# A fused decoder layer on one core: the second feed-forward block computed with seven products in all eight row-tile pairs

## The chip, the core and the metric

The kernel runs on one core of one Trainium2 chip. The metric is the time of one execution on the device, in microseconds (us), as the median of several runs. The core has five engines with an instruction queue each, worked through in order: PE (matrix products), DVE (vector), ACT (activation, copies), POOL (GpSimd, here mostly issuing transfers) and SP (issuing transfers). An instruction that has to wait for another engine or for a transfer holds up everything behind it in its own queue.

## The reference

One decoder layer on 256 tokens of width 2048, all in float32. The change touches only the last line, the feed-forward part (`D_FF` is 5632):

```python
n = rms_norm(x, attn_norm_g)
proj = n @ w_in
...
h = x + jnp.concatenate([gla_out, nsa_out], axis=-1) @ w_out
m = rms_norm(h, ffn_norm_g)
return h + (jax.nn.silu(m @ w_gate) * (m @ w_up)) @ w_down
```

## The kernel before

**Precision.** Each float32 operand is split into two parts that the matrix unit takes: `hi`, which ACT writes by a copy, and `lo`, which DVE writes as operand minus `hi` (`in_parts`, lines 661 and 662). A product of two operands takes three matmuls: hi by hi, hi by lo, lo by hi. So every weight tile costs ACT and DVE a pass each before PE can use it.

**Feed-forward part.** The columns of `w_gate` and `w_up` are cut in 11 blocks of 512 (`FB`). The main loop (line 1424) runs `gate_up(f)` for a block and then `down(f - 1)`, the product of the block before with `w_down`; block 0 has no `down` behind it, so block 1 follows block 0 directly. The 2048 rows of the weights are 16 tiles of 128, taken as 8 pairs. A pair holds two gate tiles and two up tiles of 128 by 512, and is multiplied with two row tiles of 128 tokens. There are two ways to do that:

- Plain: 2 by 2 by 2, that is 8 products, 24 matmuls. Four weight tiles are split (one copy and one subtraction of 128 by 2048 elements).
- Seven products (a fast 2-by-2 multiplication): 21 matmuls. It needs three raw tiles split (128 by 1536), and four sums of weight tiles split (two passes of 128 by 1024 each on ACT and DVE, `parts_of2`). The token side needs sums too, the "forms", made once for each pair and kept (`pair_forms`).

**Where the four sums of a pair come from.** There are three ways. DVE makes them in the block (lines 1229 to 1231: one pass of 128 by 1024, two of 128 by 512). Or they were made early, on DVE during the earlier stages, stored in DRAM ("sums", `SUMS`), and are fetched by two POOL transfers (line 1172). Or two of the four are made by a transfer that adds (`HALVES`, `fetch_half`): POOL fetches a gate tile and an up tile into one buffer (lines 1182 and 1183), waits until both have landed, and issues a third transfer that adds the other up tile to both (line 1184); DVE makes the other two sums from the result (lines 1230 and 1231).

**Block 1 before.** `FIRST7` gives five pairs the seven products (0, 2, 3, 4, 5) and leaves 1, 6 and 7 plain; the order of pairs is 0, 1, 2, 6, 3, 4, 5, 7 (`ORDER1`). The sums of 2, 3, 4 and 5 come from DRAM, those of 0 are made on DVE. Later blocks do all eight pairs with seven products in plain order, two pairs with sums from DRAM (4 and 7), two with halves (2 and 6). The seven products of all pairs are summed in seven of the eight PSUM banks; plain pairs also need bank 8. So `turn_act(0)`, which transposes block 0's result for `down(0)` into a bank, uses banks 1 and 5 once these are read, after block 1's last seven-product pair; in later blocks it uses bank 8 at the start of the block.

**Buffers.** Raw weights have 4 buffers (`fraw`), split weights 4 (`ftwo`, two for a seven-product pair), sums 3 (`fsum`). A pool of 24 buffers, `g4`, holds everything else: 4 for the residual `h`, 8 for the tokens in two parts, one for the forms of each pair (6 before block 1; pairs 6 and 7 follow during block 1, `late_forms`, with a scratch buffer each), 2 for the transposed result of a block, and what is left serves sums from DRAM, halves, and sums made on DVE in blocks 0 and 1. A scheduler places the instructions of the program on the five queues; it interleaves pairs where operands are late. Transfers of a half keep the written order.

Of the kernel before, what the change touches and what calls it, by code (L numbers as in the profile page):

```python
# [37 lines left out]
def kernel(  # L38
# [986 lines left out]

    PAIRS7, FIRST7 = tuple(range(8)), {0: (0, 2, 4), 1: (0, 2, 3, 4, 5)}

    EARLY7 = (0,1,2,3,4,5)  # L1030
# [157 lines left out]
    def gate_up(fb):  # L1188
# [9 lines left out]
            assert k in turned  # L1198
            return tuple(x[k // 4][:, k % 4, t * P:(t + 1) * P] for x in (hT_h, hT_l))

        order, sevens = (ORDER0, ORDER1, ORDER)[min(fb, 2)], FIRST7.get(fb, PAIRS7)
        last7 = max(sevens, key=order.index)
        todo = dict.fromkeys((1, 5, 6, 7), 3 * len(sevens))
        todo.update(dict.fromkeys((2, 3, 4), 3 * len(sevens) + 6 * (8 - len(sevens))))
        todo[8] = 6 * (8 - len(sevens))
        total = dict(todo)
        if fb > 1:
            urgent.append(turn_act(fb - 1, (8, 8)))
        for at, pair in enumerate(order):
# [44 lines left out]
            if pair == last7:  # L1254
                (q1, q7u), (u, q5u), (q57u, _) = ((t[:, 0], t[:, 1]) for t in (fw["sum"]([2, 512]) for _ in range(3)))
                act(q1, banks[1], AF.Copy)
                TT(u, banks[6], q1, ALU.add)  # L1257
                TT(q5u, banks[5], u, ALU.subtract)
                TT(q7u, banks[7], u, ALU.add)
                TT(q57u, banks[5], q7u, ALU.subtract)  # L1260
                if fb == 1:
                    urgent.append(turn_act(0, (1, 5)))
                if fb:
                    seed(0, DOWN[min(fb - 1, 1)])
        if fb == 0:
            drain(urgent)
            rms(rf, ssh)
# [35 lines left out]

    DOWN = ((6, 7), (2, 3), (6, 7), (4, 8)), ((1, 6), (7, 5), (2, 3), (4, 1))

    def seed(n, qs):
        for t in range(NT):
            last["seed", n] = nc.scalar.copy(banks[qs[n][t]], h_sb[n][:, t, :])  # L1310

    def down(f):
        ah, al = acts.pop(f)
        qs = DOWN[min(f, 1)]
        for n in range(4):
            bs = [banks[q] for q in qs[n]]
            ws = parts_of(load4([(w_down[0], 4 * f, 4, n * 512)]), last["seed", 0] if n == 2 and f else None)
            if n < 3 and (f or n != 1):
                seed(n + 1, qs)
# [145 lines left out]
```

## Time and profile before

| | |
|---|---|
| median of 3 runs | 1095.55 us (1095.54 to 1096.16) |
| profiled execution, its own time | 1095.91 us |
| its span, first to last instruction | 1094.2 us |
| PE busy | 1088.2 us, 99% |
| DVE busy | 988.4 us, 90% |
| ACT busy | 764.7 us, 70% |
| POOL busy | 129.2 us, 12% |
| granted TensorE clock | 1.000 |

The profile is of one execution. A group row names line, engine, operation, output and inputs, shape and count, then busy time, mean duration of one in ns, and the idle time before it with what ended it. A windows row gives each engine's busy time in a stretch of the span and the number of instructions in brackets, the clock, the busy share of the DMA engines and what they moved. A timeline row gives start, duration, engine and instruction; neighbours of a kind are merged.

### The profile page before, as it was taken

How to read it: one execution, taken by the hardware profiler on the slowest of the kernel's cores; microseconds unless marked ns; L12 is line 12 of the kernel's file. 1: busy time of each engine (PE TensorE's matmuls, PEld its weight loads, DVE VectorE, ACT ScalarE, POOL GpSimd, SP SyncE). 2: the span in 40 equal slices, each digit the busy share in tenths (PEclk: the TensorE clock that was granted, in tenths of full speed). 3: DMA queues.
4: the chain of work that ended last, by engine and by line, in shares of the span. 5: the costliest groups of instructions: out<-in, count | busy, mean ns of one | idle time of the engine just before them, and what ended most of it. 6: DMA issues, size and time to landing. Idle time of an engine off the chain costs nothing.

```text
span 1094.2 us, 14835 instructions
## 1 busy us (share of the span) xinstructions
PE 1088.2 (99%) x5256; PEld 895.3 (82%) x5256; DVE 988.4 (90%) x1316; ACT 764.7 (70%) x1060; POOL 129.2 (12%) x213
## 2 busy tenths in 40 slices
PE   9999999999999999999999999999999999999998
PEld 8888888987878877888888888888888887888877
DVE  6768879987799888997999999999999999999997
ACT  7745557555687586677686967777686877777695
POOL 4100001032110100010101011010101011110100
PEclk9999999999999999999999999999999999999999
DMA  7999978468876947696787969787797869788862
GB/s 278 357 356 350 398 251 295 166 232 287 308 274 252 342 153 287 216 336 208 250 278 221 299 200 302 246 266 236 261 288 236 280 207 288 227 279 255 247 231 78
DMA packets 135272, 287.76 MB, mean 263 GB/s; under 512 B 8135, under 2 KB 10219, under 8 KB 135197
## 3 DMA queue, kind: packets, MB, share of 16 engines
q1 hardware_dynamic: 112844, 218.17, 57.4%
q0 software_dynamic: 21744, 68.17, 20.4%
q8 instruction: 41, 0.67, 0.2%
q10 hardware_dynamic: 608, 0.47, 0.1%
q14 instruction: 35, 0.28, 0.1%
HBM read 263.71 MB, written 23.07 MB: 262 GB/s over the span
## 4 chain that ended last, share of the span: by engine, by line
PE 85%; DVE 6%; issue 3%; ACT 2%; DMA 2%; POOL 1%; SPq 0%; DVEq 0%; POOLq 0%; ACTq 0%
PE bank L297 41%; PE bank L1194 37%; PE bank L215 3%; PE bank L1339 2%; DVE lo L145 2%; PE bank L977 1%; DMA fraw<-in_w_up_dram 1%; DMA g<-in_w_up_dram 1%; POOL sm L218 1%; DMA sums<-g 1%; ACT g L912 1%; DVE ftwo L662 0%; DVE g L1115 0%; ACT hi L144 0%; PE bank L899 0%
## 5 line engine op out<-in xcount | busy, mean ns | idle before, releaser
L1194 PE MATMUL bank<-ftwo,g 128*128 128x512 f32 x1824 | 427.1, 393 | 0.5 <-ACT ftwo L661 0.2
L1194 PEld LDWEIGHTS bank<-ftwo,g 128*128 128x128 f32 x1824 | 337.2, 188 | 77.5 <-ACT ftwo L661 3.2
L297 PE MATMUL bank<-hi,g 128*128 128x512 f32 (+1 forms) x1088 | 320.9, 376 | 0.4 <-ACT g L912 0.4
L662 DVE TENSOR_TENSOR ftwo<-fraw,ftwo 128x1536 fp32r<-128x1536 f32 (+1 forms) x130 | 253.0, 1952 | 4.7 <-ACT ftwo L661 4.7
L661 ACT ACTIVATE ftwo<-fraw 128x1536 fp32r<-128x1536 f32 (+1 forms) x130 | 212.5, 1641 | 17.5 <-PE bank L1194 14.4
L297 PE MATMUL bank<-ftwo,g 128*128 128x512 f32 x960 | 221.6, 391 | 0.0
L297 PEld LDWEIGHTS bank<-hi,g 128*128 128x128 f32 x1088 | 191.5, 188 | 31.0 <-issue 1.0
L297 PEld LDWEIGHTS bank<-ftwo,g 128*128 128x128 f32 x960 | 179.3, 188 | 39.5 <-ACT bank L1310 1.2
L297 PE MATMUL bank<-lo,g 128*128 128x512 f32 (+3 forms) x544 | 193.0, 375 | 0.1
L144 ACT ACTIVATE hi<-raw 128x1024 fp32r<-128x1024 f32 (+3 forms) x124 | 130.5, 1059 | 82.8 <-PE bank L297 56.0
L145 DVE TENSOR_TENSOR lo<-raw,hi 128x1024 fp32r<-128x1024 f32 (+3 forms) x124 | 150.2, 1219 | 30.3 <-ACT hi L144 29.7
L661 ACT ACTIVATE ftwo<-fsum 128x1024 fp32r<-128x1024 f32 x118 | 121.9, 1054 | 70.6 <-DVE fsum L1229 53.6
L662 DVE TENSOR_TENSOR ftwo<-fsum,ftwo 128x1024 fp32r<-128x1024 f32 x118 | 142.0, 1221 | 13.7 <-ACT ftwo L661 13.7
L297 PEld LDWEIGHTS bank<-lo,g 128*128 128x128 f32 x544 | 98.2, 189 | 14.5 <-DVE lo L145 0.3
L661 ACT ACTIVATE ftwo<-g 128x1024 fp32r<-128x1024 f32 x46 | 48.7, 1059 | 35.8 <-PE bank L1194 23.3
L1322 ACT COPY g<-bank 128x512 f32<-128x512 f32 x80 | 45.6, 583 | 27.8 <-PE bank L297 26.4
L662 DVE TENSOR_TENSOR ftwo<-g,ftwo 128x1024 fp32r<-128x1024 f32 x46 | 56.2, 1221 | 2.2 <-ACT ftwo L661 2.2
L1119 POOL DMA_DIRECT2D sums<-g x40 | 21.8, 545 | 260.1 <-DVE g L1115 206.3
L1310 ACT COPY bank<-g 128x512 f32<-128x512 f32 x80 | 45.1, 589 | 7.6 <-DVE fsum L1257 6.2
L1229 DVE TENSOR_TENSOR fsum<-fraw 128x1024 f32<-128x1024 f32 x36 | 44.0, 1223 | 0.1
L215 PE MATMUL bank<-ident,g 128*128 128x128 f32 (+3 forms) x232 | 42.6, 277 | 0.6 <-ACT g L912 0.5
L1231 DVE TENSOR_TENSOR fsum<-fsum,fraw 128x512 f32<-128x512 f32 x60 | 41.4, 689 | 1.0
(251 smaller groups left out, 951.8 us busy)
## 6 DMA issues: line engine op xcount, KB each, us to landing
fraw<-in_w_gate_dram SPq DMA_DIRECT2D x86, 512.0 KB, 4.4
fraw<-in_w_down_dram SPq DMA_DIRECT2D x42, 1024.0 KB, 6.8
raw<-in_w_in_dram SPq DMA_DIRECT2D x36, 1024.0 KB, 6.1
fraw<-in_w_up_dram SPq DMA_DIRECT2D x45, 512.0 KB, 5.4
sums<-g POOLq DMA_DIRECT2D x40, 512.0 KB, 6.6
raw<-in_w_out_dram SPq DMA_DIRECT2D x16, 1024.0 KB, 8.5
g<-in_w_up_dram POOLq DMA_DIRECT2D x21, 512.0 KB, 7.6
fraw<-in_w_up_dram SPq DMA_DIRECT2D x41, 256.0 KB, 4.3
```

Of the source, the lines that this page charges most:

```text
L144: act(h[:, i:i + n], r[:, k + i:k + i + n], AF.Copy)
L145: last["d"] = TT(o[:, i:i + n], r[:, k + i:k + i + n], f32(h[:, i:i + n]), ALU.subtract)
L215: return nc.tensor.transpose(o, i, ident[:n, :n])
L297: last["mm"] = mm(bk[t], a[:, k, t * P:(t + 1) * P], ws[k][m][:, off:off + w], start=(first_ and k == 0 and i == 0), stop=(end and k == 3 ...
L661: act(hi, ps, AF.Copy)
L662: last["d"] = TT(lo, ps, f32(hi), ALU.subtract)
L1194: mm(banks[q], x, m, start=todo[q] == total[q], stop=todo[q] == 1)
L1229: TT(s1, r[:, 1:3], r[:, 3:4].to_broadcast([P, 2, 512]), ALU.add)
L1231: TT(s2[:, 1], s2[:, 0], r[:, 0], ALU.add)
L1310: last["seed", n] = nc.scalar.copy(banks[qs[n][t]], h_sb[n][:, t, :])
L1322: nc.scalar.copy(h_sb[n][:, t, :], bs[t])
L1339: mm(bk, u, m, start=(first and i == 0), stop=(end and i == 2), skip_group_check=onto)
```

## The change

Block 1 does all eight pairs with seven products, in the plain order 0 to 7. Its four sums in DRAM are those of pairs 2, 4, 5 and 7 (before: 2, 3, 4, 5). Pairs 3 and 6 get halves by adding transfers; 0 and 1 are made on DVE. Bank 8 is free in block 1 then, and so `turn_act(0)` moves to the start of block 1, and `down(0)` uses the same banks as later `down`s, with their way of seeding a bank with the residual. The rest of the diff takes out what only block 1 needed.

```diff
-    PAIRS7, FIRST7 = tuple(range(8)), {0: (0, 2, 4), 1: (0, 2, 3, 4, 5)}
+    PAIRS7, FIRST7 = tuple(range(8)), {0: (0, 2, 4)}
...
-    HALVES = {f: (2, 6) if f < 8 else (2, 4, 6) for f in range(2, NFB)}
+    HALVES = {f: (3, 6) if f == 1 else (2, 6) if f < 8 else (2, 4, 6) for f in range(1, NFB)}
...
-    ORDER1 = (0,1,2,6,3,4,5,7)
...
-    SUMS[1] = (2, 3, 4, 5)
+    SUMS[1] = (2, 4, 5, 7)
...
-        if fb > 1:
-            urgent.append(turn_act(fb - 1, (8, 8)))
+        if fb:
+            urgent.append(turn_act(fb - 1))
...
-                if fb == 1:
-                    urgent.append(turn_act(0, (1, 5)))
                 if fb:
-                    seed(0, DOWN[min(fb - 1, 1)])
+                    seed(0)
...
-            p = banks[qs[t]]
+            p = banks[8]
...
-    DOWN = ((6, 7), (2, 3), (6, 7), (4, 8)), ((1, 6), (7, 5), (2, 3), (4, 1))
+    DOWN = (1, 6), (7, 5), (2, 3), (4, 1)
```

Three places show how instructions move. In the rows, `[waits ...]` names the engines and transfer queues whose semaphores the instruction waits for. First POOL's queue in block 1, before. A name such as `sums0_1_4` is the first of the two parts of the sums of block 1, pair 4, in DRAM:

```order
L1172 DMA fsum_859_4716<-sums1_1_2_750 128x1024 [waits DMASW3_49,DMASW1_49,DVE_49]
L1172 DMA fsum_870_4800<-sums1_1_3_836 128x1024 [waits DMASW4_49,DVE_49]
L1172 DMA fsum_874_4834<-sums1_1_4_927 128x1024 [waits DMASW5_49,DMASW3_49,DVE_49]
L1172 DMA g4_869_4799<-sums0_1_3_835 128x1024 [waits DMASW6_49]
L1172 DMA g4_873_4833<-sums0_1_4_926 128x1024 [waits DMASW7_49,DMASW2_49]
L1172 DMA g4_878_4869<-sums0_1_5_1044 128x1024 [waits DMASW0_49,DVE_49,PE_49]
L1172 DMA fsum_879_4870<-sums1_1_5_1045 128x1024 [waits DMASW4_49,DVE_49]
```

The same queue now, from the row behind the one that fetches the second part of pair 2's sums, which waits as before. `g4_862` is the half of pair 3, `g4_881` that of pair 6; `g4_890` and `fsum_891` are the sums of pair 7:

```order
L1181 DMA g4_862_4725<-in_w_gate_dram 128x512 [waits DMASW7_49,DMASW4_49,PE_49]
L1182 DMA g4_862_4725<-in_w_up_dram 128x512 [waits DMASW5_49]
L1183 DMA g4_862_4725<-in_w_up_dram 128x2x512 [waits DMASW6_49,DMASW5_49,DMASW4_49]
L1171 DMA fsum_874_4816<-sums1_1_4_836 128x1024 [waits PE_49]
L1171 DMA fsum_880_4855<-sums1_1_5_927 128x1024 [waits DMASW0_49,DMASW3_49,DVE_49,Activation_49]
L1171 DMA g4_873_4815<-sums0_1_4_835 128x1024 [waits DMASW2_49]
L1171 DMA g4_879_4854<-sums0_1_5_926 128x1024 [waits DMASW6_49,DVE_49]
L1181 DMA g4_881_4858<-in_w_gate_dram 128x512 [waits DVE_49]
L1182 DMA g4_881_4858<-in_w_up_dram 128x512
L1171 DMA fsum_891_4936<-sums1_1_7_1045 128x1024 [waits DVE_49]
L1183 DMA g4_881_4858<-in_w_up_dram 128x2x512 [waits DMASW4_49,DMASW3_49]
L1171 DMA g4_890_4935<-sums0_1_7_1044 128x1024 [waits DMASW7_49,DMASW1_49,DVE_49]
```

Seven transfers of sums have become seven transfers of sums with two halves of three transfers each between them. In the built program, the wait of `g4_881`'s gate tile is for the DVE instruction that ends the forms of pair 6, and that of `g4_890` for the one that ends the forms of pair 7: each takes over the scratch buffer of these forms.

Second, ACT's queue at the end of block 1, before; `ftwo` are split weights, 881 and 882 those of pair 4, 884 and 885 of pair 5, 890 the plain pair 7, 894 the first of `down(0)`:

```order
L661 ACTIVATE ftwo_882_4888<-fsum_874_4834 128x1024 [waits DMASW5_49]
L661 ACTIVATE ftwo_884_4908<-fraw_883_4905 128x1536 [waits DMAHW5_49,DMAHW6_49,PE_49,Activation_49]
L661 ACTIVATE ftwo_885_4920<-g4_878_4869 128x1024 [waits DMASW0_49,DVE_49,PE_49]
L661 ACTIVATE ftwo_885_4920<-fsum_879_4870 128x1024 [waits DMASW1_49]
L661 ACTIVATE ftwo_890_4950<-fraw_889_4947 128x2048 [waits DMAHW0_49,DMAHW7_49,DVE_49,PE_49]
L661 ACTIVATE ftwo_894_5001<-fraw_893_4999 128x2048 [waits DMAHW1_49,DVE_49,PE_49]
```

And now; 893 and 895 are pair 6, 897 and 898 pair 7, `g4_885` the forms of pair 7, 903 the first of `down(0)`:

```order
L661 ACTIVATE ftwo_893_4942<-fraw_892_4939 128x1536 [waits DMAHW5_49,DMAHW6_49,DVE_49,PE_49]
L661 ACTIVATE ftwo_895_4957<-g4_881_4858 128x1024 [waits DMASW4_49,DMASW3_49,DMASW6_49,DVE_49,PE_49]
L661 ACTIVATE ftwo_897_4977<-fraw_896_4974 128x1536 [waits DMAHW0_49,DMAHW7_49,DVE_49,PE_49]
L661 ACTIVATE g4_885_4877<-g4_884_4871 128x512 [waits DVE_49,Activation_49]
L661 ACTIVATE ftwo_898_4980<-fsum_891_4936 128x1024 [waits DMASW5_49,PE_49,Activation_49]
L661 ACTIVATE ftwo_895_4957<-fsum_894_4945 128x1024 [waits DVE_49]
L661 ACTIVATE ftwo_898_4980<-g4_890_4935 128x1024 [waits DMASW7_49]
L661 ACTIVATE ftwo_903_5025<-fraw_902_5023 128x2048 [waits DMAHW1_49,PE_49,Activation_49]
```

The copy that needs the half of pair 6 (`DMASW6` is its adding transfer) now stands ahead of the copy for the forms of pair 7.

Third, DVE's queue at the same place, before: operands of pairs 4 and 5, then plain pair 7 and `down(0)`:

```order
L662 TENSOR_TENSOR ftwo_882_4888<-fsum_874_4834,ftwo_882_4888 128x1024
L662 TENSOR_TENSOR ftwo_884_4908<-fraw_883_4905,ftwo_884_4908 128x1536
L662 TENSOR_TENSOR ftwo_885_4920<-g4_878_4869,ftwo_885_4920 128x1024
L662 TENSOR_TENSOR ftwo_885_4920<-fsum_879_4870,ftwo_885_4920 128x1024
L662 TENSOR_TENSOR ftwo_890_4950<-fraw_889_4947,ftwo_890_4950 128x2048
L662 TENSOR_TENSOR ftwo_894_5001<-fraw_893_4999,ftwo_894_5001 128x2048
```

And now, from the raw tiles of pair 6 to the last operand of pair 7:

```order
L662 TENSOR_TENSOR ftwo_893_4942<-fraw_892_4939,ftwo_893_4942 128x1536
L662 TENSOR_TENSOR g4_885_4877<-g4_884_4871,g4_885_4877 128x512
L1227 TENSOR_TENSOR fsum_894_4945<-g4_881_4858,fraw_892_4939 128x512
L662 TENSOR_TENSOR ftwo_895_4957<-g4_881_4858,ftwo_895_4957 128x1024
L1228 TENSOR_TENSOR fsum_894_4945<-fsum_894_4945,fraw_892_4939 128x512
L662 TENSOR_TENSOR ftwo_897_4977<-fraw_896_4974,ftwo_897_4977 128x1536
L662 TENSOR_TENSOR ftwo_895_4957<-fsum_894_4945,ftwo_895_4957 128x1024
L662 TENSOR_TENSOR ftwo_898_4980<-g4_890_4935,ftwo_898_4980 128x1024
L662 TENSOR_TENSOR ftwo_898_4980<-fsum_891_4936,ftwo_898_4980 128x1024
```

Three passes over 2048 elements have gone from block 1, and pairs 6 and 7 now bring small ones that depend on the half `g4_881` and on the sums `g4_890`.

More of the change, by code (lines that the diff above doesn't have):

```diff
@@ L1199, in tokens @@
             return tuple(x[k // 4][:, k % 4, t * P:(t + 1) * P] for x in (hT_h, hT_l))
-        order, sevens = (ORDER0, ORDER1, ORDER)[min(fb, 2)], FIRST7.get(fb, PAIRS7)
+        order, sevens = (ORDER0, ORDER)[min(fb, 1)], FIRST7.get(fb, PAIRS7)
         last7 = max(sevens, key=order.index)
@@ L1206, in gate_up @@
         total = dict(todo)
-        if fb > 1:
-            urgent.append(turn_act(fb - 1, (8, 8)))
+        if fb:
+            urgent.append(turn_act(fb - 1))
         for at, pair in enumerate(order):
-            if fb > 1 and pair not in sevens:
-                drain(urgent)
             if fb == 0 and at == len(OLD):
@@ L1278, with turn_act @@
     hidden, acts = {}, {}
-    def turn_act(fb, qs):
+    def turn_act(fb):
         for _ in range(2):
@@ L1300, in turn_act, with seed @@
                 pair_forms(8 + pair, v, f)
-    DOWN = ((6, 7), (2, 3), (6, 7), (4, 8)), ((1, 6), (7, 5), (2, 3), (4, 1))
-    def seed(n, qs):
+    DOWN = (1, 6), (7, 5), (2, 3), (4, 1)
+    def seed(n):
         for t in range(NT):
-            last["seed", n] = nc.scalar.copy(banks[qs[n][t]], h_sb[n][:, t, :])
+            last["seed", n] = nc.scalar.copy(banks[DOWN[n][t]], h_sb[n][:, t, :])
     def down(f):
         ah, al = acts.pop(f)
-        qs = DOWN[min(f, 1)]
         for n in range(4):
[L1316 to L1319, printed above, removed]
+            bs = [banks[q] for q in DOWN[n]]
+            ws = parts_of(load4([(w_down[0], 4 * f, 4, n * 512)]), last["seed", 0] if n == 2 else None)
+            if n < 3:
+                seed(n + 1)
             yield from chunk([bs], ah, al, ws, False, True, onto=True)
@@ L1322, in down @@
                 nc.scalar.copy(h_sb[n][:, t, :], bs[t])
-            if n == 0 and not f:
-                seed(2, qs)
     def down_last():
@@ L1430 @@
             if f == NFB - 1:
-                urgent.append(turn_act(f, (8, 8)))
+                urgent.append(turn_act(f))
             drive([down(f - 1)], 3)
```

## The prediction

> **What bounds the kernel now.** I read the page first, then the stretches of the feed-forward blocks, then the groups by shape, then the order of time around block 1.
>
> ```profile
> PE 1088.2 (99%) x5256; PEld 895.3 (82%) x5256; DVE 988.4 (90%) x1316; ACT 764.7 (70%) x1060; POOL 129.2 (12%) x213
> ...
> PE 85%; DVE 6%; issue 3%; ACT 2%; DMA 2%; POOL 1%; SPq 0%; DVEq 0%; POOLq 0%; ACTq 0%
> ```
>
> The busy row and the chain that ended last both name PE. A kernel like this gets faster only by fewer matmuls, and slower by every gap that opens between them. But DVE is close behind. The stretches show how close; they are block 1, `down(0)`, block 2 and, as a settled block, block 3:
>
> ```profile
> core 0: us, PE busy (x) PEld busy (x) DVE busy (x) ACT busy (x) POOL busy (x), PEclk, DMA share, GB/s
> ...
> 453.40:494.00 40.60, 40.60 (x183) 33.53 (x182) 37.80 (x42) 29.02 (x27) 5.99 (x10) 1.00 0.94 322
> 494.00:516.40 22.40, 22.40 (x101) 18.25 (x100) 19.09 (x19) 14.78 (x21) 0.00 (x0) 1.00 0.54 179
> 516.40:555.80 39.40, 39.40 (x178) 32.03 (x177) 37.55 (x35) 29.07 (x29) 6.55 (x10) 1.00 0.79 264
> ...
> 577.50:617.20 39.70, 39.70 (x178) 32.19 (x178) 38.84 (x37) 29.39 (x29) 6.82 (x10) 1.00 0.79 265
> ```
>
> A block of eight seven-product pairs leaves DVE 0.86 us idle of 39.70 (block 3). It holds PE's pace because the `down` before it lets DVE run ahead (3.31 us idle in 22.40 at 494). Block 1 has no `down` before it. Today its three plain pairs are what leaves DVE room: 2.80 us idle of 40.60.
>
> **The change, part by part.** First PE. Block 1 falls from 5 x 21 + 3 x 24 = 177 matmuls to 168:
>
> ```profile
> L1194 PE MATMUL bank<-ftwo,g 128*128 128x512 f32 x1824 | 427.1, 393 | 0.5 <-ACT ftwo L661 0.2 <-DVE ftwo L662 0.2
> ```
>
> Matmuls overlap, so the price of one is busy time over count, 427.1 / 1824 = 0.234 us, not the mean of 393 ns. Nine of them are 2.1 us. The eight transposes of block 0's result are only moved, four of them from `down(0)` to block 1.
>
> Second, DVE. The shapes, and how they follow each other:
>
> ```profile
> L662 DVE TENSOR_TENSOR ftwo<-fraw,ftwo 128x1536 fp32r<-128x1536 f32 x82 | 143.9, 1755 | 2.3 <-ACT ftwo L661 2.3
> L662 DVE TENSOR_TENSOR ftwo<-fsum,ftwo 128x1024 fp32r<-128x1024 f32 x118 | 142.0, 1221 | 13.7 <-ACT ftwo L661 13.7
> ...
> L661 ACT ACTIVATE ftwo<-fsum 128x1024 fp32r<-128x1024 f32 x118 | 121.9, 1054 | 70.6 <-DVE fsum L1229 53.6 <-DVE fsum L1231 11.6 <-DMA fsum<-sums 2.8
> L661 ACT ACTIVATE ftwo<-fraw 128x1536 fp32r<-128x1536 f32 x82 | 121.6, 1483 | 11.1 <-PE bank L1194 8.8 <-DMA fraw<-in_w_up_dram 1.3 <-ACT fsum L1272 0.9
> ...
> L1231 DVE TENSOR_TENSOR fsum<-fsum,fraw 128x512 f32<-128x512 f32 x60 | 41.4, 689 | 1.0
> ...
> L661 ACT ACTIVATE g<-g 128x512 fp32r<-128x512 f32 x18 | 11.2, 630 | 5.4 <-DVE g L1049 5.1
> ```
>
> ```profile
> 451.45 2.28 DVE L662 TENSOR_TENSOR ftwo<-fraw,ftwo 128x2048 fp32r<-128x2048 f32 x1
> 453.64 0.75 DVE L1275 SCALAR_TENSOR_TENSOR fsum<-fsum,rf,fsum 128x512 f32<-128x512 f32 x1
> ...
> 456.10 0.75 DVE L1275 SCALAR_TENSOR_TENSOR fsum<-fsum,rf,fsum 128x512 f32<-128x512 f32 x1
> ...
> 459.64 1.23 DVE L662 TENSOR_TENSOR ftwo<-fsum,ftwo 128x1024 fp32r<-128x1024 f32 x1
> 460.77 0.29 DVE L1046 TENSOR_TENSOR g<-g 128x128 f32<-128x128 f32 x1
> ```
>
> From start to start an instruction takes 0.09 us less than its duration (451.45 to 453.64 for 2.28). So a pass of 2048 elements costs 2.19 us, 1536 costs 1.67, 1024 costs 1.13, 512 costs 0.60, the fused multiply 0.66, a form of 128 by 128 costs 0.20. A plain pair costs DVE 2.19; a pair with sums from DRAM 1.67 + 2 x 1.13 = 3.93; a half adds two of 0.60, 5.13; sums made on DVE add 1.13 more, 6.26. Before, block 1 holds 6.26 + 4 x 3.93 + 3 x 2.19 = 28.6; now 4 x 3.93 + 2 x 5.13 + 2 x 6.26 = 38.5. That is 9.9 us more for DVE, while PE's time shrinks by 2.1, against 2.80 us of idle time. DVE does not fit.
>
> How far over, I count along DVE's new order. Up to 451.45 it is the old one. The subtraction that starts there is now one of 1536, for pair 1. From it to the last operand of pair 7 stand 7 of 1536, 16 of 1024, 16 of 512, 2 fused and 8 small forms: 11.7 + 18.1 + 9.6 + 1.3 + 1.6 = 42.3 us, so 493.8 if DVE never waits. Some six matmuls follow the last operand, 1.4 us: block 1 would end at about 495.3, where it ends at 494.0 today:
>
> ```profile
> 493.99 4.25 PE L297 MATMUL bank<-ftwo,g 128*128 128x512 f32 x18
> 498.08 0.60 PE L215 MATMUL bank<-ident,fsum 128*128 128x128 f32 x4
> 498.44 18.13 PE L297 MATMUL bank<-ftwo,g 128*128 128x512 f32 x78
> ```
>
> Third, the adding transfers, which decide it. How long POOL's chain for a half takes, from the first issue to the landing of the sum, and what sums from DRAM take:
>
> ```profile
> 477.17 0.54 POOL L1182 DMA_DIRECT2D g<-in_w_gate_dram  x1 [5.39 <-DVE ftwo L662]
> 477.70 0.54 POOL L1183 DMA_DIRECT2D g<-in_w_up_dram  x1
> 483.99 1.25 POOL L1184 DMA_DIRECT2D g<-in_w_up_dram  x1 [5.75 <-DMA g<-in_w_up_dram]
> ```
>
> ```profile
> L1184 POOL DMA_DIRECT2D g<-in_w_up_dram x21: 1202/1220/1245, 484.0 to 1023.7; - x21
> ...
> DMA to landing us min/median/max: 5.9/7.6/10.3
> ```
>
> ```profile
> L1172 POOL DMA_DIRECT2D g<-sums x20: 527/558/582, 418.5 to 1016.1; - x20
> ...
> DMA to landing us min/median/max: 3.6/6.3/9.5
> ```
>
> The adding transfer is issued 6.8 us after the first (477.17 to 483.99) and lands 7.6 later: 14.4 us; the bounds are 6.8 + 5.9 = 12.7 and 6.8 + 10.3 = 17.1. Sums take 6.3, from 3.6 to 9.5. The Trainium skill, "DMA: Bandwidth & Descriptors", section "Anatomy of one DMA — SWDGE (gpsimd) path", gives such a transfer 2.0 us plus its bytes at 436 GB/s: as an estimate 2.6 us for 256 KB and 3.2 for 512 KB, 5.8 for a half and 3.2 for sums. By these the chain below would be 11.7 us shorter and would end before DVE does. The rows here take two to two and a half times that, with other queues moving data too, and I go by the rows.
>
> In settled blocks 14 us is hidden, because the buffer for a half is free a block ahead. In block 1 it is not. The `g4` pool has 24 buffers. 4 + 8 + 6 are held at its start, 2 now go to block 0's transposed result at once, and 4 remain, for the sums of pairs 0 and 1, those of pair 2 from DRAM and the half of pair 3. Each of the two late forms keeps one more for good and needs a scratch one. So the half of pair 6 can only be requested when DVE has ended the forms of pair 6, and the sums of pair 7 only when it has ended those of pair 7, which on ACT stand behind the copies of pair 6's half. Step by step:
>
> - Forms of pair 6 end on DVE. Along DVE's order 3 of 1536, 7 of 1024, 12 of 512, 2 fused, 4 forms: 5.0 + 7.9 + 7.2 + 1.3 + 0.8 = 22.2, so 473.7. Two waits come on top. The second transposes of block 0's result stand on PE behind pair 1's sums: I estimate 0.6. The half of pair 3 stands on POOL behind a fetch that waits for the fused multiply which ends at 456.85: issued at about 457.1, landed at 471.5, its copy of 1.05 delays DVE by 1.2. 475.5.
> - The half of pair 6: 14.4 gives 489.9.
> - ACT, in order, copies it (1.05), the raw tiles of pair 7 (1.48) and the forms of pair 7 (0.63), 0.1 less each by overlap: 2.9, 492.8. DVE subtracts (0.69), 493.5.
> - The sums of pair 7: 6.3, 499.8; their copy 1.05, 500.9.
> - PE's order has 19 matmuls from the first that needs them to the end of the block: 4.4, 505.3.
> - Then `down(0)` needs bank 1 seeded, behind two more copies on ACT: I estimate 0.8, bounds 0 and 2. The four transposes at 498.08 are no longer there: 498.08 to 498.44, less 0.4. Net 505.7.
>
> Against 494.0 that is 11.7 us later; the nine matmuls saved are inside, since PE waits. From there on block 2 has what it had: DVE's 3.3 us of idle time in `down(0)` refills its lead, and no later row is touched. What POOL's queue holds behind the two waits is block 2's first half, issued some ten us later than now but still ahead of a block that starts as much later.
>
> **The sum.** The profiled execution took 1095.91 us for a span of 1094.2, 0.36 over the median of 1095.55. I put 11.7 on the median: 1107.2 us. With the fastest rows (12.7 and 3.6) the chain is 4.4 shorter, 1102.8; with the slowest (17.1 and 9.5) 5.9 longer, 1113.1.
>
> **The rivals.** About 0.2%, 2.2 us, is what a measurement of this kernel can tell from no change.
>
> DVE alone decides (0.17). Its place is block 1, its price the 1.3 us of the order count, plus up to 3 us where DVE waits for ACT and PE in turn, less 0.4: about 2.4 later, 1098.0 us, from 1096.4 to 1099.5. It decides when the half of pair 6 and the sums of pair 7 together land at least 9 us sooner than in my rows. For it: block 1 carries less traffic per us when it lasts longer, and its share of DMA time today is 0.94, the highest of the rows above. By the rule of the Trainium skill named above, this case is what comes out. Against it: no half in the trace went below 5.9 us for its last transfer alone.
>
> The work is hidden, and only the matmuls count (0.08). Place: block 1 on PE, price nine matmuls at 0.234, 2.1 us less, 1093.4 us. It decides if DVE's lead at the start of block 1 covers 9.9 us more work. For it: DVE works ahead today, its pass at 451.45 is already for pair 1, while block 1 begins on PE at 453.4. Against it: the order count, which contains this lead, ends after 494.0.
>
> The transfers crowd each other (0.07). Two pairs that fetched four tiles of 256 KB, 6 and 7, now fetch seven, in a block that already has a DMA share of 0.94. If the slowest rows hold for both waits, the time is above 1113.1.
>
> That the change does not do what it says can be left out: PE's new order has 168 matmuls in block 1.
>
> **How the numbers follow.** The chain through pairs 6 and 7 gets 0.68. Slower by over 0.2%: 0.68 + 0.07 and 0.12 of DVE alone, 0.87. Within: the other 0.05 and a part of the hidden case, whose 2.1 us lies at the edge, 0.07. Faster: 0.06. The range takes in the DVE case from its middle, 1098.0, to just below the slowest rows, 1113.0.
>
> **What would show it.** In the new profile, block 1 from its first matmul to `down(0)` should last about 52 us with some 39.5 of matmuls in it, and PE's gaps should lie near its end. ACT's waits should show one on the half of pair 6 and one on pair 7's sums (`g` from `sums`), several us each; POOL should issue the third transfer of the second half at about 482 and pair 7's sums at about 493. Blocks 2 to 10 should keep 39.6 us. I am wrong if ACT waits for neither transfer, or if block 1 ends before 497.

## The result, and the profile after

The changed kernel takes 1108.67 us (1107.97 to 1109.69, 4 runs) against 1095.55 (1095.47 to 1096.16, 4 runs): 1.0119 times as long, with a 95% interval of 1.0102 to 1.0137. The profiled execution took 1108.36 us, for a span of 1106.6.

First the busy row of the page and the chain that ended last:

```profile
PE 1091.8 (99%) x5247; PEld 895.7 (81%) x5247; DVE 997.9 (90%) x1328; ACT 769.0 (69%) x1066; POOL 134.2 (12%) x219
...
PE 77%; issue 11%; DVE 5%; ACT 3%; DMA 3%; POOL 2%; ACTq 0%; DVEq 0%; POOLq 0%
```

Nine matmuls are gone and PE is still called busy 99% of the time, so the busy row hides the loss; only the chain moves, with "issue" (time in which an engine waited for nothing that the profile shows) at 11% where it was 3%. The stretches show where. Their columns are as in the prediction; the rows are block 1, `down(0)`, and block 2 as a settled block:

```profile
453.60:506.60 53.00, 44.19 (x178) 33.79 (x176) 43.19 (x49) 30.41 (x30) 9.49 (x15) 0.94 0.78 246
506.60:529.00 22.40, 22.40 (x99) 18.39 (x99) 22.27 (x22) 17.19 (x24) 1.22 (x1) 1.00 0.85 263
529.00:568.60 39.60, 39.60 (x179) 32.13 (x178) 38.74 (x36) 29.38 (x29) 6.83 (x10) 1.00 0.80 266
```

Block 1 lasts 53.0 us where it lasted 40.6. `down(0)` and block 2 last what they did. All of the loss lies in block 1, and in it PE and DVE both stand idle, 8.8 and 9.8 us. That is the mark of a wait for something that is neither of them. PE's order of time around the two holes (the brackets give the idle time and what ended it):

```profile
474.01 16.20 PE L1193 MATMUL bank<-ftwo,g 128*128 128x512 f32 x63 [3.51 <-ACT ftwo L661]
494.60 5.55 PE L1193 MATMUL bank<-ftwo,g 128*128 128x512 f32 x15 [4.39 <-ACT ftwo L661]
500.66 6.06 PE L1193 MATMUL bank<-ftwo,g 128*128 128x512 f32 x24 [0.50 <-ACT ftwo L661]
506.70 5.51 PE L297 MATMUL bank<-ftwo,g 128*128 128x512 f32 x23
```

ACT ended both holes, with the copies of the two halves, and it had waited itself. (The 0.50 us at 500.66 are for its copy of pair 6's last sums.) Its waits by what ended them (total, times, longest), and in the order of time the copies of half 3, of half 6, of the last sums of pair 6 (from DVE) and of pair 7's sums:

```profile
ACT ftwo L661 <- DMA g<-in_w_up_dram: 16.4, 2, 9.4
```

```profile
472.90 1.06 ACT L661 ACTIVATE ftwo<-g 128x1024 fp32r<-128x1024 f32 x1 [7.06 <-DMA g<-in_w_up_dram]
...
493.49 1.06 ACT L661 ACTIVATE ftwo<-g 128x1024 fp32r<-128x1024 f32 x1 [9.38 <-DMA g<-in_w_up_dram]
...
499.54 1.06 ACT L661 ACTIVATE ftwo<-fsum 128x1024 fp32r<-128x1024 f32 x1 [2.15 <-DVE fsum L1228]
501.01 1.06 ACT L661 ACTIVATE ftwo<-g 128x1024 fp32r<-128x1024 f32 x1 [0.40 <-DMA g<-sums]
```

POOL's queue tells when each was asked for: the first load of a half (L1181), the adding transfer of the second (L1183), and at 497.47 pair 7's sums. The row at 418.53 is the last thing that POOL does ahead of block 0, and is used below as a common zero:

```profile
418.53 0.70 POOL L218 TENSOR_TENSOR rf<-fm,mhalf 128x2 f32<-128x2 f32 x1 [41.03 <-DVE fm L282]
...
457.47 0.54 POOL L1181 DMA_DIRECT2D g<-in_w_gate_dram  x1
...
477.82 0.54 POOL L1181 DMA_DIRECT2D g<-in_w_gate_dram  x1 [1.47 <-DVE g L662]
...
483.91 1.21 POOL L1183 DMA_DIRECT2D g<-in_w_up_dram  x1 [3.39 <-issue]
...
497.47 0.57 POOL L1171 DMA_DIRECT2D g<-sums  x1 [12.34 <-DVE g L662]
```

Half 3 takes 15.4 us from its request to the end of ACT's wait (457.47 to 472.90), half 6 takes 15.7 (477.82 to 493.49). The second is asked for only after DVE has ended the forms of pair 6, a chain with the first inside it.

One thing was not foreseen. Here are a stretch behind each hole and one between them, 3 us each:

```profile
474.70:477.70 3.00, 3.00 (x9) 2.32 (x8) 1.51 (x2) 3.00 (x5) 0.53 (x1) 0.50 0.96 354
480.00:483.00 3.00, 3.00 (x15) 2.47 (x14) 3.00 (x4) 2.35 (x4) 0.52 (x1) 1.00 0.82 246
...
495.00:498.00 3.00, 3.00 (x9) 2.32 (x8) 1.52 (x3) 2.39 (x3) 0.53 (x1) 0.50 0.00 0
```

For some 3.4 us behind each hole the granted clock (third from the right) is 0.50, and 9 matmuls fall into 3 us instead of 15. From one start to the next the trace has 427 ns there, and 227 elsewhere.

### The profile page after: what moved, and what is told of

The parts are those of the page before. It is cut to its first block, busy times and chain, and to the rows that moved or that the text cites. A ratio compares the mean times of both kernels' runs of the same rounds, so it can differ in the third digit from the quotient of the medians.

```text
span 1106.6 us, 14860 instructions
## 1 busy us (share of the span) xinstructions
PE 1091.8 (99%) x5247; PEld 895.7 (81%) x5247; DVE 997.9 (90%) x1328; ACT 769.0 (69%) x1066; POOL 134.2 (12%) x219
## 4 chain that ended last, share of the span: by engine, by line
PE 77%; issue 11%; DVE 5%; ACT 3%; DMA 3%; POOL 2%; ACTq 0%; DVEq 0%; POOLq 0%
PE bank L297 39%; PE bank L1193 32%; PE bank L215 2%; DMA g<-in_w_up_dram 2%; PE bank L1331 2%; DVE lo L145 2%; PE bank L977 1%; POOL sm L218 1%; ACT g L912 1%; DMA g<-in_w_gate_dram 0%; ACT hi L144 0%; POOL sc L218 0%; PE bank L899 0%; ACT ftwo L661 0%; PE bank L205 0%
## 5 line engine op out<-in xcount | busy, mean ns | idle before, releaser
L661 ACT ACTIVATE ftwo<-fraw 128x1536 fp32r<-128x1536 f32 (+1 forms) x130 | 210.9, 1630 | 14.4 <-PE bank L1193 12.9
L661 ACT ACTIVATE ftwo<-fsum 128x1024 fp32r<-128x1024 f32 x121 | 125.0, 1054 | 73.5 <-DVE fsum L1226 56.2
L662 DVE TENSOR_TENSOR ftwo<-fsum,ftwo 128x1024 fp32r<-128x1024 f32 x121 | 145.6, 1220 | 11.8 <-ACT ftwo L661 11.8
L661 ACT ACTIVATE ftwo<-g 128x1024 fp32r<-128x1024 f32 x49 | 51.8, 1058 | 51.2 <-PE bank L1193 22.7
L662 DVE TENSOR_TENSOR ftwo<-g,ftwo 128x1024 fp32r<-128x1024 f32 x49 | 59.8, 1220 | 1.0 <-ACT ftwo L661 1.0
L1183 POOL DMA_DIRECT2D g<-in_w_up_dram x23 | 28.0, 1220 | 128.6 <-DMA g<-in_w_up_dram 101.9
```

Of the source, the lines that this page charges most:

```text
L661: act(hi, ps, AF.Copy)
L662: last["d"] = TT(lo, ps, f32(hi), ALU.subtract)
L1183: tc.keep_in_program_order(nc.gpsimd.dma_start(s1, b, accum_op=ALU.add))
```

## The experiments

In the expectations I took this theory: block 1 is long because the two halves land late, and by the slow matmuls behind the holes on top. The rivals were DVE's added work (the halves then only show it), and DMA bandwidth. The kernels of each group ran beside the kernel before on one chip; its median was 1095.41 to 1095.51.

**No halves, and one half.** The edits are of one table:

```diff
-    HALVES = {f: (3, 6) if f == 1 else ...
+    HALVES = {f: () if f == 1 else ...        (e1)
+    HALVES = {f: (6,) if f == 1 else ...      (e2)
```

> Block 1 without adding transfers: the sums of pairs 3 and 6 are made on DVE, as pairs 0 and 1 have them; everything else as in the changed kernel. Theory (the two halves land late, PE stands 3.9 and 4.8 us for them, and its matmuls run slower for some 4 us behind each): both gaps go, and block 1 ends where DVE's order ends, 493.8 + 2 x 1.13 for the two sums + 1.4, so about 497.5 on the old clock of the span, 3.1 us behind the kernel before: 1098.6 us, from 1098 to 1101. Rival 1 (DVE's 9.9 us of added work is the loss, and the halves only show it): 2.3 us more than the changed kernel's 1108.7, so 1111. Rival 2 (block 1 is short of DMA bandwidth): 1.5 MB less is moved, at the 247 to 322 GB/s of this stretch 4.7 to 6.1 us, so 1103 to 1104, with DMA busy to the end of the block.

> Only pair 6 of block 1 keeps its adding transfer; pair 3's sums are made on DVE. Theory: the first gap of 3.9 us goes with the slow matmuls behind it, DVE gets 1.1 us more, the forms of pair 6 end near 475 where they ended at 477.8, the half that waits for them lands near 490 to 491 where it landed at 493.4, and PE still stands for it, longer than the 4.8 us before, since it gets there sooner. The time falls by the 3 us by which this half lands sooner: 1105.7 us, from 1104 to 1107. If the two gaps were independent of each other: 3.9 + 1.7 - 1.1 less, 1104. Rival 1 (DVE's work): 1109.8.

Without halves: 1100.43 us (1.0046, 1.0031 to 1.0061), inside the range that the theory gave. DVE has 2.3 us more work than in the changed kernel, and the kernel is 8.2 us faster; so DVE's work is not what cost most. What remains, 5.0 us over the kernel before, goes with it. The first and second part of block 1 in this kernel:

```profile
453.10:475.80 22.70, 20.58 (x91) 15.58 (x90) 22.66 (x28) 13.79 (x15) 2.65 (x5) 1.00 0.62 233
475.80:498.40 22.60, 20.85 (x88) 15.73 (x87) 22.39 (x23) 16.05 (x16) 3.38 (x5) 1.00 0.80 277
```

DVE is busy 45.05 of 45.30 us (its column is the fourth), PE has the idle time, and the DMA engines have room. With half 6 alone: 1104.79 us (1.0086, 1.0071 to 1.0101), inside what the theory gave; but PE stood 2.91 us for the half, where I had expected more than 4.8. POOL's and ACT's rows of this kernel:

```profile
417.30 0.70 POOL L218 TENSOR_TENSOR rf<-fm,mhalf 128x2 f32<-128x2 f32 x1 [41.01 <-DVE fm L282]
...
473.92 0.54 POOL L1181 DMA_DIRECT2D g<-in_w_gate_dram  x1 [1.28 <-DVE ftwo L662]
```

```profile
489.69 1.06 ACT L661 ACTIVATE ftwo<-g 128x1024 fp32r<-128x1024 f32 x1 [6.31 <-DMA g<-in_w_up_dram]
```

**Asking sooner, with the same work.** In block 1 two statements change places, so that a half is asked for ahead of the sums of the pair before; in the second kernel the late forms' scratch also leaves the pool of 24 buffers:

```diff
+            if fb == 1 and at < 6 and order[at + 2] in HALVES[1]:
+                fetch_half(fb, order[at + 2])
             if at < 7:
                 fetch_sums(fb, order[at + 1])
-            if at < 6 and order[at + 2] in HALVES.get(fb, ()):
+            if fb != 1 and at < 6 and order[at + 2] in HALVES.get(fb, ()):
                 fetch_half(fb, order[at + 2])
...
-                v, f = form_tiles()                                   (e4 only)
+                v, f = g2([2, S]), banks[8].rearrange("p (a b) -> p a b", a=4)
```

> POOL asks for a half of block 1 ahead of the sums of the pair before it instead of behind them: two statements change places, for block 1 alone. The half of pair 3 no longer stands behind a fetch that waits for block 0's last fused multiply, and should be asked for before block 1 starts. The half of pair 6 then takes the buffer of that of pair 3. Theory: gap one and its slow matmuls go, 5.6 us; the half of pair 6 is asked for when DVE has read that of pair 3, near 471, lands near 486, and PE, which wants it near 484, waits about 2 us: 1100 to 1101.5 us. Rivals 1 and 2 (DVE's work, bandwidth): no work is taken away, 1108 to 1109.

> As the kernel with the two statements exchanged, and the two late forms have their scratch outside the pool of 24 buffers: v in the one buffer of f2, f in the idle bank 8. The half of pair 6 then waits for no buffer, only for its place on POOL behind the sums of pair 5, whose buffer comes free when pair 2 is subtracted, near 466. Theory: it lands near 481, before PE wants it, both gaps and the slow matmuls go, and what is left is DVE's order, 495.3 with no wait, less 0.4 for the transposes: 1096.5 to 1099 us. Rivals 1 and 2: 1108 to 1109, since DVE and the DMA engines do the same work.

The first: 1105.26 us (1.0091, 1.0073 to 1.0108), slower than I expected by 4. Half 3 was asked for at 418.90 and cost nothing any more, but half 6 was asked for at 472.24, not near 471, and took 16.8 us, not 15:

```profile
417.15 0.70 POOL L218 TENSOR_TENSOR rf<-fm,mhalf 128x2 f32<-128x2 f32 x1 [41.01 <-DVE fm L282]
...
472.24 0.54 POOL L1181 DMA_DIRECT2D g<-in_w_gate_dram  x1 [4.14 <-DVE ftwo L662]
```

```profile
489.08 1.06 ACT L661 ACTIVATE ftwo<-g 128x1024 fp32r<-128x1024 f32 x1 [7.03 <-DMA g<-in_w_up_dram]
```

The second: 1101.36 us (1.0061, 1.0044 to 1.0078), 2.4 over the upper end of what I gave:

```profile
417.28 0.70 POOL L218 TENSOR_TENSOR rf<-fm,mhalf 128x2 f32<-128x2 f32 x1 [40.99 <-DVE fm L282]
...
468.19 0.54 POOL L1181 DMA_DIRECT2D g<-in_w_gate_dram  x1
```

```profile
486.37 1.06 ACT L661 ACTIVATE ftwo<-g 128x1024 fp32r<-128x1024 f32 x1 [5.71 <-DMA g<-in_w_up_dram]
```

Half 6 took 18.2 us there, so it still came late: PE stood 2.59 us for it. Asked for sooner, it shared the DMA engines with the sums of pairs 4 and 5, and the engines were busy all the time (second number from the right):

```profile
469.00:477.00 8.00, 7.14 (x30) 5.00 (x29) 8.00 (x12) 5.83 (x6) 2.55 (x4) 1.00 1.03 376
```

To this extent the rival of crowded transfers fits; no run tests it by itself.

The four kernels give the cause, by one number each of their profiled executions. Counted from POOL's `rf` row to the end of the wait for half 6, it is 74.96 us in the changed kernel, 72.39 with half 6 alone, 71.93 asked sooner, 69.09 with the scratch moved. From the same row to the end of the span (1106.6, 1102.7, 1102.1, 1098.4) it is 688.1, 685.4, 684.9 and 681.1. Against the changed kernel the half lands 2.6, 3.0 and 5.9 us sooner, and the program ends 2.7, 3.1 and 7.0 sooner. The landing of half 6 sets the end of block 1. The last kernel gains 1.1 us more than its landing explains. In it pair 7's sums no longer wait for a buffer: they are asked for at 482.01, ahead of half 6's landing, where the changed kernel asks at 497.47, behind it. That this is the 1.1 us is not shown. That two of these kernels do exactly the work of the changed one shuts out DVE's work as the cause of this part. What ACT's order adds, with the copy of the half ahead of pair 7's forms, no run here changes.

**The clock.** 35 matmuls that nothing reads, into the idle bank 8:

```diff
+                    if fb == 1 and q == 5 and pair in FILL:
+                        for _ in range(FILL[pair]):
+                            mm(banks[8], hT_h[0][:, 0, :P], hT_h[0][:, 0:2].rearrange("p a b -> p (a b)"), start=True, stop=True)
...
+    FILL = {3: 17, 6: 18}
```

> The changed kernel with 35 matmuls more in block 1, hT_h against itself into the idle bank 8, whose result nothing reads: 13 ahead of or inside the first gap, 1 and 3 places earlier 4 more that the order puts where PE is close to waiting, and 18 inside the second gap. No wait and no transfer is touched. Theory (the matmuls 427 ns apart behind each gap are a lower granted clock that follows from PE standing still for 3.9 and 4.8 us): with the gaps filled up to some 0.7 us, the matmuls behind them go 228 ns apart, and 1.7 + 1.5 = 3.2 us come back: 1105.5 us, from 1105 to 1107 where a filler runs past the end of its gap. Rival (the slow matmuls have another cause, such as operands that come late or DMA traffic): they stay 427 ns apart, and the time is 1108.7 or up to 1 more.

1110.82 us (1.0142, 1.0125 to 1.0159): 2.2 more than the changed kernel, and a miss for the price that I had put on the clock. The time of the first hole, and the 3 us where the slow matmuls had been:

```profile
470.20:474.20 4.00, 4.00 (x18) 3.03 (x17) 2.54 (x5) 2.43 (x3) 0.00 (x0) 1.00 1.04 390
474.90:477.90 3.00, 1.46 (x6) 0.63 (x4) 1.94 (x3) 2.87 (x5) 1.39 (x3) 1.00 1.01 358
```

With the hole filled the clock stays at 1.00, so it did follow from PE standing still. But the time that it costs there was never lost: PE runs into the wait for half 6 in any case, and half 6 lands when POOL and DVE let it: with the fillers 75.19 us behind the `rf` row (417.61 to 492.80), in the changed kernel 74.96. In the same way PE at the slow clock behind the second hole of the changed kernel still runs into a wait for ACT, at 500.66, and reaches the product of pair 7's sums just as their copy ends, at 502.07 (501.01 + 1.06); faster, it would have waited longer there. Behind the second hole the fillers put PE's products in another order, a new hole of 2.7 us opened, with the clock at 0.50 for 6.8 us behind it, and that half of the test says nothing.

So the slow clock was measured by itself, in the kernel before, in block 4, where nothing is late. One matmul, eight (or four) settings of its operand to zero on POOL, one matmul more:

```diff
+                    if fb == 4 and q == 5 and pair == 3:
+                        t = g2([512], F32R)
+                        nc.gpsimd.memset(f32(t), 0.0)
+                        a = mm(banks[8], hT_h[0][:, 0, :P], t, start=True, stop=True)
+                        with behind(a):
+                            for _ in range(8):
+                                nc.gpsimd.memset(f32(t), 0.0)
+                            last["gap"] = mm(banks[8], hT_h[0][:, 0, :P], t, start=True, stop=True)
...
-                mm(banks[q], x, m, start=todo[q] == total[q], stop=todo[q] == 1)
+                with behind(last.get("gap") if fb == 4 else None):
+                    mm(banks[q], x, m, start=todo[q] == total[q], stop=todo[q] == 1)
```

> The kernel before, with PE made to stand still once in block 4, where DVE, ACT and the transfers are ahead: ahead of the first product of pair 3 that needs sums, one matmul into the idle bank 8, then eight settings of its operand to zero on POOL, 0.55 us each by the row of such a one, then one more matmul. Nothing is left out, and no operand of the block is late. PE stands for 8 x 0.5 + 0.4, about 4.4 us, and has 0.5 us of added matmuls. Theory (a stop of this length lowers the granted clock for some 4 us, whatever it was that PE waited for): about ten matmuls 427 ns apart follow, 2.0 us: 1102.3 us, from 1101.5 to 1103. Rival (in the changed kernel late operands made the matmuls slow): 228 ns apart, 1100.3 us.

> The same with four settings: PE stands for about 2.3 us. Gaps of 1.9 to 3.1 us were followed by slow matmuls in some of the kernels run here and not in others. Theory without the clock: 1095.4 + 2.3 + 0.5 = 1098.2 us; with a lower clock behind it, 7 matmuls by 0.2, 1099.6. A stop of half the length should cost less than half of what the longer one costs, if the clock has a part in it that the short stop escapes.

Eight: 1107.34 us (1.0108, 1.0093 to 1.0123). Four: 1102.68 us (1.0062, 1.0045 to 1.0078). Both cost far more than I gave, and the short stop costs more than half of the long one (7.2 and 11.8 us). The 3 us behind the stop with eight settings, then with four:

```profile
661.00:664.00 3.00, 3.00 (x9) 2.27 (x9) 1.93 (x3) 0.00 (x0) 1.62 (x4) 0.55 0.66 208
```

```profile
659.50:662.50 3.00, 3.00 (x9) 2.31 (x8) 2.97 (x3) 0.00 (x0) 0.70 (x2) 0.55 1.00 373
```

PE's waits say how long the stops were, with eight and with four:

```profile
PE bank L1245 <- POOL f L1244: 4.7, 1, 4.7
PE bank L1195 <- DVE ftwo L662: 2.0, 1, 2.0
```

```profile
PE bank L1245 <- POOL f L1244: 2.4, 1, 2.4
```

The clock falls behind a stop of 4.7 us and behind one of 2.4, with no weights late: seven or eight matmuls at some 427 ns, 1.4 to 1.6 us. What I had not seen is that my settings stand in POOL's queue ahead of the half of pair 6. POOL with eight settings, then the kernel before, then ACT with eight:

```profile
655.89 4.61 POOL L1244 MEMSET f<- 128x512 f32 x8 [12.28 <-PE bank L1241]
660.48 0.55 POOL L1182 DMA_DIRECT2D g<-in_w_gate_dram  x1
```

```profile
647.85 0.55 POOL L1182 DMA_DIRECT2D g<-in_w_gate_dram  x1 [3.47 <-DVE ftwo L662]
```

```profile
674.54 1.06 ACT L661 ACTIVATE ftwo<-g 128x1024 fp32r<-128x1024 f32 x1 [5.68 <-DMA g<-in_w_up_dram]
```

The half is asked for 12.6 us late, lands 14.1 us after that, and PE stands 2.0 us more, the second row of its waits above, with slow matmuls again behind it. Of the 11.8 us, 4.7 are the stop, 2.0 the second one, 3.0 some fifteen slow matmuls by 0.2, 0.5 the two added ones; the other 1.6 I did not trace. With four settings the half is asked for 10.7 us late (658.59), and PE stands 1.2 and 0.6 us more, without a second fall of the clock. It repeats the cause of block 1 in a block where halves are hidden.

**Can block 1 bear eight sevens at all?** Five versions looked for one that beats both kernels. Six stored sums instead of halves; half 3 alone, asked for sooner; the same with all forms early; the same with the small additions of pairs 4 to 7 on POOL; and the kernel before with a sixth pair in sevens.

```diff
-    HALVES = {f: (3, 6) if f == 1 else ...
-    SUMS[1] = (2, 4, 5, 7)
+    HALVES = {f: () if f == 1 else ...
+    SUMS[1] = (2, 3, 4, 5, 6, 7)
```

```diff
-    HALVES = {f: (3, 6) if f == 1 else ...
+    HALVES = {f: (3,) if f == 1 else ...
...
-    EARLY7 = (0,1,2,3,4,5)
+    EARLY7 = (0,1,2,3,4,5,6,7)
...
+        TF = nc.gpsimd.tensor_tensor if 4 <= pair < 8 else TT
```

The first is e6. Of the second, with the exchange of the two statements above, e7 has the first piece, e8 the first two, and e9 all three, TF taking the place of TT in the four additions of `pair_forms`. The last, e10, is cut from the kernel before:

```diff
-    PAIRS7, FIRST7 = tuple(range(8)), {0: (0, 2, 4), 1: (0, 2, 3, 4, 5)}
+    PAIRS7, FIRST7 = tuple(range(8)), {0: (0, 2, 4), 1: (0, 1, 2, 3, 4, 5)}
-    HALVES = {f: (2, 6) if f < 8 else (2, 4, 6) for f in range(2, NFB)}
+    HALVES = {f: (2, 6) if f < 7 else (2, 4, 6) for f in range(2, NFB)}
-    ORDER1 = (0,1,2,6,3,4,5,7)
+    ORDER1 = (0,6,2,1,3,4,5,7)
-    SUMS = {f: (4, 7) if f < 8 else (7,) for f in range(2, NFB)}
-    SUMS[1] = (2, 3, 4, 5)
+    SUMS = {f: (4, 7) if f < 7 else (7,) for f in range(2, NFB)}
+    SUMS[1] = (1, 2, 3, 4, 5)
```

> Block 1 with no adding transfer: all of the pairs 2 to 7 have their sums from DRAM, six stored sums instead of four, so two more are made in the attention stages. DVE in block 1 has 2 x 1.2 us less than with halves: its order ends at 491.4, the block at 492.8 by DVE and at 453.4 + 39.4 + 0.4 = 493.2 by PE. Theory (late halves, then DVE's order, are all that holds block 1): 1095.5 us, from 1094 to 1097, if the two more sums cost nothing in the stages ahead, where DVE is idle 12 us of 50 at 250, up to 5 us more if they do. Rival (DMA bandwidth): as many bytes as with halves are read in block 1, so it would stay above 1100, with ACT waiting for sums of pairs 5 to 7.

> Block 1 with one half, that of pair 3, asked for ahead of the sums of pair 2; pair 6's sums are made on DVE. The half was asked for at 419 and landed at 438 in the kernel with both halves and the same exchange, so nothing waits for it. Theory: DVE has 1.13 us less than with both sums made on it, which took 1100.4: 1099.3 us, from 1098.3 to 1100.3, with no gap over 2 us on PE and no slow matmuls. Rival (each half costs a wait of its own): 1102 or more.

> As the kernel with one half asked for sooner, and the forms of pairs 6 and 7 are made where those of pairs 0 to 5 are, ahead of block 0, instead of in block 1: EARLY7 holds all eight. In block 1 DVE loses the two sums of hi and lo, eight forms and two subtractions, 2 x (0.6 + 4 x 0.2 + 0.6) = 4.0 us; ahead of block 0, where it is idle 6.5 us from 400 to 420, it gets 2.8. Two more buffers of the 24 are held, which leaves two for stored sums beside the half. Theory (DVE's order is what is left of the loss): 493.8 + 1.1 - 4.0 + 1.4 = 492.3, below what PE needs, 453.4 + 39.4 + 0.4 = 493.2: 1094.8 us, from 1093.8 to 1096.5, the only version so far that could be as fast as the kernel before or faster. Rival (the buffers decide): stored sums are asked for later and ACT waits for them, 1098 or more.

> As the kernel with all eight forms early, and the 16 small additions of the forms of pairs 4 to 7 are made on POOL, which is idle there from 376 to 417, instead of on DVE. That kernel gains in block 1 what it should, and loses 2.5 us to two gaps in block 0 at 422 and 424, where ACT and DVE come late with the operands of block 0. Theory (DVE's room ahead of block 1 is what is short): DVE gets 16 x 0.20 = 3.2 us back between 395 and 425, the two gaps shrink from 1.2 and 1.0 us to the 0.4 and 0.1 that the kernel before has there, and the time falls from 1097.4 to 1095.4 us, from 1094.5 to 1096.5, level with the kernel before. Rival (POOL's small operations are so slow, or so much in DVE's way, that the last forms come late): 1097 to 1099.

> The kernel before with six pairs of block 1 in seven products instead of five: pair 1 too, with its sums from DRAM and fourth in the order, after the plain pair 6. Block 7 gives up the stored sums of pair 4 for an adding transfer, so that as many sums are stored as before; no adding transfer in block 1, and no form is early or late that was not. Theory (what a block bears in sevens is set by DVE's room): PE has 3 matmuls less, 0.7 us; DVE has 3.93 - 2.19 = 1.74 us more of the 2.80 us that it has idle in block 1, so nothing waits for it: 1094.8 us, from 1094.2 to 1096. Rival (each further pair costs a wait for its sums whatever DVE has left): 1097 or more. If it comes out level with the kernel before, the two hardly tell apart.

Six stored: 1103.09 us (1.0073, 1.0051 to 1.0095), a miss. POOL's `rf` row comes 2.4 us later than in the changed kernel, so the two more sums made in the stages ahead are not free. In block 1 PE waits 2.2 us in one piece for DVE, and ACT waits three times for stored sums:

```profile
420.97 0.71 POOL L218 TENSOR_TENSOR rf<-fm,mhalf 128x2 f32<-128x2 f32 x1 [23.15 <-DVE fm L282]
```

```profile
PE bank L1193 <- DVE ftwo L662: 2.2, 1, 2.2
```

```profile
ACT ftwo L661 <- DMA g<-sums: 7.5, 2, 5.5
ACT ftwo L661 <- DMA fsum<-sums: 3.7, 1, 3.7
```

The rival had named both signs, a time above 1100 and ACT waiting for sums. That does not make bandwidth the cause: ACT's longest wait, up to 493.35, is for sums that POOL asked for at 487.81, 5.5 us before, in a queue that had stood 7.4 us for DVE. The DMA engines were 0.96 busy meanwhile. This run does not tell the late request from the crowded engines.

Half 3 alone, sooner: 1098.88 us (1.0031, 1.002 to 1.0041), as the theory gave. All forms early: 1097.41 us (1.0019, 1.001 to 1.0029), a miss by 2.6. PE hardly waits in block 1 any more; the loss moved to block 0. Here are 6 us of block 0 and 39 of block 1 in this kernel, and then the same 6 us in the kernel before:

```profile
420.00:426.00 6.00, 4.11 (x15) 2.39 (x14) 5.78 (x7) 4.96 (x5) 1.29 (x4) 1.00 1.05 413
456.00:495.10 39.10, 38.46 (x171) 30.52 (x169) 38.08 (x36) 28.66 (x27) 4.83 (x9) 1.00 0.84 302
```

```profile
420.00:426.00 6.00, 5.76 (x25) 4.38 (x25) 5.74 (x5) 3.81 (x3) 0.09 (x1) 1.00 1.05 415
```

DVE is as busy as before in those 6 us, with the same work of block 0, but 1.6 us later: the forms ahead of it end at 419.1 (418.41 + 0.69) instead of 417.5 (416.77 + 0.69). 15 matmuls fall into the 6 us instead of 25. This profiled execution is the fastest of ten (1096.54 us, granted clock 1.000); the six slowest, 1097.07 to 1099.42, have a mean granted clock of 0.998, so part of the loss of the median seems to go with the clock. On POOL the forms are worse: 1104.23 us (1.0088, 1.0072 to 1.0104), beyond the range of the theory and of the rival. An addition of 128 by 128 that takes DVE 0.29 us (460.77 in the prediction's rows) takes POOL 0.45 to 1.32:

```profile
409.00 1.32 POOL L1049 TENSOR_TENSOR g<-g,g 128x128 f32<-128x128 f32 x1
```

From 395 to 435, ACT waits 6.2 us for what comes of them, and DVE 9.7 us for ACT (3.7 in the kernel before). The `rf` row comes at 426.74, 7.3 us later than with all forms on DVE (419.46), and the granted clock is 0.50 from 429.3 to 436.0. That is the rival's mechanism, larger than I had priced it.

The sixth seven: 1098.2 us (1.003, 1.0021 to 1.0039), 2.8 slower than the kernel before with three matmuls less. PE's and ACT's waits in block 1 and the start of `down(0)`:

```profile
PE bank L297 <- DVE g L662: 0.9, 1, 0.9
PE bank L1194 <- DVE ftwo L662: 0.8, 1, 0.8
PE bank L297 <- ACT g L661: 0.4, 1, 0.4
```

```profile
ACT ftwo L661 <- DMA fsum<-sums: 7.3, 4, 2.7
```

ACT waits four times for stored sums, 2.7 us at most, and hands it on to DVE and PE. The kernel before has such waits too, three that make 3.8 us, 2.6 at most, and its PE does not stop in block 1; here they are 3.5 us more. That speaks for the rival: a further pair cost a wait for its sums, though DVE has room (2.08 us idle in the 41.00 from 453). That PE's waits come from ACT's is read from the order of the engines; no run tests it. The span of its profiled execution, 1095.9, is 1.7 us longer than before, and these waits of PE make 2.1 less 0.7 for the matmuls of it. No version beat the kernel before.

## Why the prediction was right

The forecast was 1107.2 us by the chain through the two halves; 1108.67 was measured. One caution on the times below: in the changed kernel's profile the `rf` row stands 0.7 us later than in that of the kernel before (418.53 and 417.82), and the DVE pass from which the prediction counts 0.3 later (451.76 and 451.45), ahead of all that the chain names. Point by point:

- **PE and DVE by count.** Nine matmuls less, as counted; DVE's added 9.9 us came out as 9.5 on the page (988.4 to 997.9). DVE alone was put at 1098.0. Half 3 alone asked sooner has 1.13 us of DVE work on top and took 1098.88; no halves at all has 2.26 on top and took 1100.43. Both come down to about 1098. The price of this rival fits; it is what is left when no half is late.
- **The forms of pair 6** end on DVE at 477.5 (the profile's row is at 476.83), not 475.5. What came on top of the count of 473.7 is 3.8 us instead of 0.6 + 1.2, 0.3 of it from the later start: the half of pair 3 was there at 472.9, 1.4 later than I had it, and behind it ACT copied raw tiles and pair 3's other sums ahead of the forms.

```profile
476.83 0.69 DVE L662 TENSOR_TENSOR g<-g,g 128x512 fp32r<-128x512 f32 x1 [1.31 <-ACT g L661]
...
496.48 0.69 DVE L662 TENSOR_TENSOR g<-g,g 128x512 fp32r<-128x512 f32 x1 [6.52 <-ACT g L661]
```

- **The half of pair 6** took 15.7 us, not 14.4, inside the bounds of 12.7 and 17.1; it was at ACT at 493.5 instead of 489.9. This is the term that decides, as the landings of the three kernels show.
- **ACT's three copies and DVE's subtraction** were right: 493.49 to 496.48 is 3.0 (2.9), then 0.69.
- **The sums of pair 7** took 3.5 us (497.47 to 501.01), not 6.3, just under the lower bound. I had named several us of waiting for them on ACT; it was 0.4. That term was mis-sized, and its part in the chain is small: ACT was busy until 500.6 (499.54 + 1.06) with pair 6's last sums, which had waited for DVE, so with the sums of pair 7 at once the block would have ended 0.4 us sooner at most. Two late things lay side by side: it was pair 6's last sums, behind half 6 on DVE and ACT, that PE waited for at 500.66.
- **The end**: `down(0)` at 506.70, forecast 505.3 + 0.8 (the transposes come later): 3.6 us too early on the half, 2.8 too long on the sums. The errors nearly cancelled, which is luck, so the closeness of the total is better than that of its parts.
- **What would show it**: a block of about 52 us with gaps near its end. It is 53.0, with one gap there; the other, at 470, stands in the middle, for half 3, which I had as 1.2 us on DVE and nothing on PE.
- **Crowded transfers**: not in the block as a whole (DMA share 0.78, where it was 0.94), but for half 6 when it is asked for sooner, 18.2 us.
- **The page's price for transfers.** The Trainium skill, "DMA: Bandwidth & Descriptors", section "Anatomy of one DMA — SWDGE (gpsimd) path", gave, as an estimate, 5.8 us for a half and 3.2 for sums. The halves of block 1 that were waited for took 15.4 to 18.2. The sums of pair 7 agree with it, 3.5, and they moved almost alone: in these 3.5 us the DMA engines moved 169 GB/s, 0.59 MB, and the sums are 0.52 MB (512 KB) of it.

```profile
497.50:501.00 3.50, 3.00 (x11) 1.81 (x9) 3.50 (x4) 1.06 (x1) 1.61 (x3) 0.88 0.60 169
```

## What to carry to other kernels

A transfer that is hidden in the settled blocks is hidden by when it is asked for, not by how long it takes: look in the first block for the buffer and for the place in its queue that hold the request back, and add up from there. Where every engine is near its limit, saved matmuls are worth only what the engine that feeds them has to spare, and moving that engine's work ahead moves the wait with it. Before a slow stretch is priced, ask what PE would have waited for at its end.

## What the runs showed of the hardware

Behind many stops of PE here the granted clock is 0.50 for about 3.4 us (6.8 behind that of 4.59 in the kernel that asks sooner), and a matmul of 128 by 512 starts every 427 ns instead of every 227. It followed the stops of 3.5 us and more here, and those of 2.9 (half 6 alone), 2.4 (four settings), 2.2 (six stored sums) and 2.0 (the second one with eight), but not that of 2.59 in the profiled execution of the kernel with the scratch moved. Two stops of 1.54 and 0.53 us, 1.3 apart, were followed by it with half 6 alone; without halves the same two, 1.55 and 0.53, were not. So the length alone does not decide. The Trainium skill, "TensorE: Matmul & The Clock Gate", section "Part 1: The HAM clock gate (the "warmup" mystery)", gives half the clock after an idle window of 3.4 us that runs by itself, and the same 427 ns; the step and the length of the slow stretch agree, but here stops shorter than the window were enough.
